# An encoder layer on one core: TensorE in source order through the projection, mixers in fewer visits, first gates fetched early

## The chip, the cores and the metric

The kernel runs on one core of one Trainium2 chip. The metric is device time in microseconds of one execution; lower is better. A core has five engines that each run their own list of instructions in order: TensorE (PE, matrix products and transposes, with PEld for the loads of the stationary operand), VectorE (DVE), ScalarE (ACT), GpSimd (POOL) and SyncE (SP, which here issues nearly all DMA transfers). They wait for each other by semaphores.

## The reference

One hybrid layer on T = 1024 tokens of width D = 1024, in float32. All weights are inputs.

```python
hn  = rms_norm(x, norm_mix_pre)
proj = hn @ w_in                       # a_qk a_v a_o a_gates | b_q b_k b_v b_r b_lr
# group A, 4 mLSTM heads: silu(dwconv3(a_qk)) gives q, k; gates i, f; one scan forward, one backward, summed
y_a = sigmoid(a_o) * head_rms_norm(h_fw + h_bw)
# group B, 4 GLA heads: decay per key dimension, log_sigmoid(b_lr @ gla_w2 + gla_b) / 16; forward and backward, summed
y_b = silu(b_r) * head_rms_norm(o_fw + o_bw)
x = x + rms_norm(concat(y_a, y_b) @ w_out, norm_mix_post)
hn = rms_norm(x, norm_ffn_pre)
g = dwconv3(hn @ w_gate, conv_w, conv_b)
x = x + rms_norm((gelu(g) * (hn @ w_up)) @ w_down, norm_ffn_post)
```

## The kernel before

**Stages.** Every float32 product is made of three float32r products of high and low halves (xh·wh, xl·wh, xh·wl). The program has four stages: the input is normalised and transposed, with a first small projection (`vacc`, L262); then the rest of the input projection with both mixers woven in; then the out-projection with the norms (`oacc`, L1002); then the gated MLP by Strassen-like products (`pr`, L1063 and L1221). The change is to the second stage alone, which begins at 47.4 us, after the eight transposes `sacc` (L283).

**The projection** is a generator, `proj`. Its unit is a block of 24 matmuls of 512 columns (`f_block`, tile `facc`, L171) or 48 matmuls of 256 columns (`t_block`, tile `tacc`, L182); a block yields after every 6 or 12 matmuls, and one such piece is called a step here. In order it makes the keys and queries of group B (`facc`), the second half of its values (`tacc`), queries and keys of group A with their convolution on ACT and DVE (`facc`), the values of group A (`tacc`), and then the two output gates, `in_gate` (`tacc`), which go to the DRAM arrays `dG` (tokens 0–511 and 512–1023). Weights come as `wraw` by SP and are split by ACT and DVE, one group of columns ahead (`ahead`). Flags in `done` ("bq", "bv", "aqk", "av", "gate") tell the mixers what is there.

**The mixers** are the other generator, `mix`. The sequence is cut into 8 chunks c of 128 tokens. `gla_decay` makes the decays of group B (8 matmuls `z`, L382, each from the split weights `w2r` and the rows `lrx`). `gate_rows` makes the gates of group A, and ends in transposes `ptc` (L373). `gla`: for each chunk `levels` forms the products of queries and keys inside it at eight distances L = 64, 32, 16, 8, 4, 2, 1, 0 (`sc`); for each level POOL makes exponents (`D`), ACT the exponential (`E`), DVE the weighted queries and keys (`Q`, `K`, `kz`), PE the small products, and DVE or ACT collects them (`acc`, `Pt`). `states` makes the running states (transpose `ptk`, product `U`, then DVE steps through `slots`, L537). `finish` makes the output of a chunk (`o`, L699 and L700), which ACT copies to `ob`, and SP stores to `dyb`. `mlstm` does the same for group A: `states` (load `kk`, transpose `ptm` L738, product `Um` L762, DVE steps `both_step`), `decays` (loads of `RB`, `RI`, then POOL and ACT), `front` (product `sr` L797, then DVE `RB` L798) and `back` (`nd`, L807 and L811; output stored to `dya`).

**The end of the stage.** After the last chunk `out_weights` loads the 8 row blocks of `w_out` (`oraw`, L862) through three buffers with the tags yv, yv, gv, and splits each on ACT and DVE (`woh`, `wol`). Then `prep(0)` loads the gated outputs of the first 128 tokens into buffers of the same tags (`yv` from `dya` and `dyb`, L875 and L876; `gv` from `dG`, L878), multiplies them on DVE (L882), and transposes them on PE (`pt`, L888), from which the out-projection starts.

**What sets the order.** Both generators only emit instructions; `_interleave` emits the next piece of the one that has run up less weight. The scheduler of the Tile framework then takes every engine's instructions, PE's too, by priority and by its own estimate of when their operands are ready, so that emitted order and final order differ. Pools of buffers (`ps` 3, `pe` 2 and `mm` 3 banks of PSUM, and pools in SBUF) add waits for a buffer's earlier readers.

Of the kernel before, what the change touches and what calls it, by code (L numbers as in the profile page):

```python
# [36 lines left out]
W_PROJ = 0.25  # L37
R_AUX, R_COLS, R_GLA, R_STATES, R_ML, R_OUT = 3.4, 0.6, 0.7, 0.7, 1.9, 2.0
# [4 lines left out]
def _interleave(*gens):  # L43
    live = [[g, w, 0.0] for g, w in gens]
    while live:
        e = min(live, key=lambda v: v[2])
        e[2] += e[1]
        try:
            w = next(e[0])
            if w is not None:  # L50
                e[1] = w
        except StopIteration:
            live.remove(e)
# [3 lines left out]
def tile_encoder_layer(  # L57
# [243 lines left out]

    def gate_rows():
# [26 lines left out]
        rm = rw.tile([R, NC, P], F32, name="rm")  # L329
        nc.gpsimd.memset(rb, 0.0)  # L330
# [38 lines left out]
        yield  # L369
        for c in range(NC):  # L370
# [4 lines left out]
            yield R_COLS * W_PROJ  # L375
        yield R_AUX * W_PROJ
# [93 lines left out]
    def in_gate(c0, off, silu):  # L470
        for g in range(2):
            wh, wl = ready.pop(0)
            yield
            for q in range(4):
# [10 lines left out]
                if q % 2:  # L485
                    nc.sync.dma_start(dG[q // 2].rearrange("(t p) n -> p t n", p=P)[:, :, off + 256 * g:off + 256 * g + 256], s)
                yield
# [11 lines left out]
    def mix():  # L499
        yield R_AUX * W_PROJ  # L500
        yield from gla_decay()
        yield from gate_rows()
        rctx.close()
        while "bq" not in done:
            yield
        gp = mctx.enter_context(tc.tile_pool(name="gp", bufs=2, reuse_waits="tile"))
        mslots = gp.tile([P, NC, H, P + 1], F32, name="mslots", bufs=1)
# [4 lines left out]

        nc.gpsimd.memset(mslots[:, 0], 0.0)
# [35 lines left out]
        def gla():  # L549
# [22 lines left out]

            def states():
                for c in range(NC):
                    S = lp.tile([P, H, P + 1], F32, name="S")
                    nc.sync.dma_start(S, dS[c // 4][c % 4])
                    kk = load(lp, "kk", dkk[c])
                    v = v_tile(lp, dvb, c)
                    nc.scalar.activation(gam[:, c, :], S[:, :, P], AF.Exp, scale=1.0 / TEMP)
                    E = edge_decay(S, hi, lo)  # L580
                    kd = w2k("Q", 3)
                    nc.vector.tensor_tensor(out=kd, in0=E, in1=kk, op=ALU.mult)
                    yield
                    pt = ps.tile([P, H, P], F32, name="ptk", tag="ps")
                    for h in range(H):
                        nc.tensor.transpose(pt[:, h, :], kd[:, h, :], ident)
# [268 lines left out]
    def out_weights():  # L855
# [11 lines left out]
        for _ in prep(0):  # L867
            pass
# [446 lines left out]
```

## Time and profile before

| | |
|---|---|
| median of 3 runs | 1193.14 us (1188.0 to 1194.34) |
| the profiled execution | 1189.67 us, span 1187.9 us |
| mean granted TensorE clock | 0.989 of full |
| PE busy | 1151.1 us, 97% of the span |
| DVE, ACT, POOL busy | 878.7, 591.4, 166.5 us |
| the stage that the change touches | 47.4 to 439.5 us |

The profile has one row for each group of instructions or, in its timeline, one for each instruction or run of like instructions: start in us, duration, engine, line, operation, `out<-in`, and in square brackets the idle time before it with what ended it. A matmul's row is longer than its pitch, since matmuls overlap: the distance of two starts is what one costs. "PEclk" is the clock that the throttle granted, where 1.00 is full.

### The profile page before, as it was taken

The page shows a single profiled execution, that of the slowest core. Times are in us where ns is not written, and L with a number is a line of the kernel's source. Part 1 is how long each engine was busy: PE and PEld are TensorE (multiplying, and loading weights), DVE is VectorE, ACT ScalarE, POOL GpSimd, SP SyncE. Part 2 cuts the span into 40 slices and gives each one's busy share as a digit, 9 for nine tenths or more (in the row PEclk, how much of TensorE's full clock was granted, in tenths as well). Part 3 has the DMA queues.
Part 4 walks back from the last instruction along what each step waited for, and adds up shares of the span by engine and source line. Part 5 has one row for each costly group of instructions (what it writes and reads, how often), then busy time and mean ns, then how long its engine had stood idle before and what let it go on. Part 6 is the DMA issues. An engine that isn't in the chain of part 4 may idle for free.

```text
span 1187.9 us, 21230 instructions
## 1 busy us (share of the span) xinstructions
PE 1151.1 (97%) x7896; PEld 979.7 (82%) x7896; DVE 878.7 (74%) x1604; ACT 591.4 (50%) x1271; POOL 166.5 (14%) x240
## 2 busy tenths in 40 slices
PE   8999999999999969999999999999999999999997
PEld 7989778888989968878788888888888878888885
DVE  5676669777433557667998888888888877987666
ACT  6572686878556534446543243433433245445451
POOL 1200425665054200101000000000000000000001
PEclk9999999999989989999999999999999999999999
DMA  7453675554777385542144342333224238754245
GB/s 201 149 134 102 169 223 155 152 171 127 189 197 209 117 278 186 178 141 80 36 142 142 109 132 64 113 123 108 89 81 133 98 123 299 252 178 133 81 137 190
DMA packets 134651, 175.77 MB, mean 148 GB/s; under 512 B 24964, under 2 KB 89860, under 8 KB 134548
## 3 DMA queue, kind: packets, MB, share of 16 engines
q1 hardware_dynamic: 134116, 172.58, 47.3%
q0 software_dynamic: 432, 1.84, 0.4%
q8 instruction: 62, 1.02, 0.3%
q14 instruction: 41, 0.34, 0.1%
HBM read 126.78 MB, written 47.53 MB: 147 GB/s over the span
## 4 chain that ended last, share of the span: by engine, by line
PE 73%; DVE 7%; ACT 6%; DMA 6%; issue 3%; POOL 3%; SPq 1%; DVEq 0%; POOLq 0%; ACTq 0%
PE pr L1063 35%; PE pr L1221 17%; PE facc L171 5%; PE oacc L1002 4%; PE tacc L182 4%; PE vacc L262 2%; DMA qq<-dmqq 1%; DMA yv<-dya 1%; DMA oraw<-in_w_out_dram 1%; DVE kz L637 1%; ACT sq L543 1%; DVE slots L537 1%; POOL RB L786 1%; POOL D L621 1%; POOL D L622 1%
## 5 line engine op out<-in xcount | busy, mean ns | idle before, releaser
L1063 PE MATMUL pr<-T,ah 128*128 128x512 f32 x704 | 217.2, 389 | 1.3 <-DVE G L1101 1.3
L1063 PE MATMUL pr<-B,ah 128*128 128x512 f32 x528 | 162.8, 390 | 0.0
L1063 PEld LDWEIGHTS pr<-T,ah 128*128 128x128 f32 x704 | 132.1, 188 | 29.4 <-DVE G L1101 1.8
L1063 PE MATMUL pr<-T,al 128*128 128x512 f32 x352 | 137.0, 389 | 0.0
L182 PE MATMUL tacc<-wh,xh 128*128 128x256 f32 x448 | 130.5, 291 | 0.0
L182 PE MATMUL tacc<-wl,xh 128*128 128x256 f32 x448 | 130.0, 290 | 0.0
L182 PE MATMUL tacc<-wh,xl 128*128 128x256 f32 x448 | 127.1, 284 | 0.0
L1221 PE MATMUL pr<-dwl,dah 128*128 128x512 f32 x308 | 120.0, 390 | 0.7 <-DVE dwl L113 0.7
L1221 PE MATMUL pr<-dwh,dal 128*128 128x512 f32 x308 | 120.1, 390 | 0.0
L1221 PE MATMUL pr<-dwh,dah 128*128 128x512 f32 x308 | 119.3, 390 | 0.0
L1063 PEld LDWEIGHTS pr<-B,ah 128*128 128x128 f32 x528 | 99.0, 188 | 20.4
L1063 PE MATMUL pr<-B,al 128*128 128x512 f32 x264 | 102.7, 389 | 0.0
L112 ACT CAST dah<-ar 128x512 fp32r<-128x512 f32 x77 | 47.6, 621 | 98.0 <-PE pr L1221 44.2
L182 PEld LDWEIGHTS tacc<-wh,xh 128*128 128x128 f32 x448 | 85.5, 191 | 2.7 <-issue 0.2
L182 PEld LDWEIGHTS tacc<-wl,xh 128*128 128x128 f32 x448 | 85.5, 191 | 1.4
L182 PEld LDWEIGHTS tacc<-wh,xl 128*128 128x128 f32 x448 | 85.7, 191 | 0.3
L112 ACT CAST ah<-fraw 128x512 fp32r<-128x512 f32 x64 | 39.6, 619 | 82.7 <-PE pr L1063 49.7
L113 DVE TENSOR_TENSOR dal<-ar,dah 128x512 fp32r<-128x512 f32 x77 | 53.0, 690 | 37.0 <-ACT dah L112 36.7
L1063 PEld LDWEIGHTS pr<-T,al 128*128 128x128 f32 x352 | 66.1, 188 | 13.6
L112 ACT CAST ah<-sa 128x512 fp32r<-128x512 f32 x44 | 27.4, 622 | 83.6 <-DVE sa L943 52.9
L1221 PEld LDWEIGHTS pr<-dwl,dah 128*128 128x128 f32 x308 | 57.8, 188 | 13.1 <-DVE dwl L113 1.1
L1221 PEld LDWEIGHTS pr<-dwh,dal 128*128 128x128 f32 x308 | 57.8, 188 | 12.9 <-DVE dal L113 0.9
(292 smaller groups left out, 2536.0 us busy)
## 6 DMA issues: line engine op xcount, KB each, us to landing
ar<-dA SPq DMA_DIRECT2D x77, 256.0 KB
wraw<-in_w_in_dram SPq DMA_DIRECT2D x48, 256.0 KB
fraw<-in_ffn_w_gate_dram SPq DMA_DIRECT2D x22, 512.0 KB
fraw<-in_ffn_w_up_dram SPq DMA_DIRECT2D x22, 512.0 KB
dA<-s SPq DMA_DIRECT2D x20, 512.0 KB
dA<-sx SPq DMA_DIRECT2D x10, 768.0 KB
Y<-in_ffn_w_down_dram SPq DMA_DIRECT2D x22, 256.0 KB
S<-dS SPq DMA_DIRECT2D x16, 258.0 KB
```

The lines of the kernel that those rows point to most:

```text
L112: nc.scalar.copy(out=hi, in_=src)
L113: nc.vector.tensor_tensor(out=lo, in0=src, in1=hi.bitcast(F32), op=ALU.subtract)
L171: nc.tensor.matmul(acc, w[:, k, cs], v[:, k, hs], start=(k == 0 and n == 0), stop=(k == NK - 1 and n == 2))
L182: nc.tensor.matmul(acc[:, i, :], v[:, k, ts], w[:, k, :], start=(k == 0 and n == 0), stop=(k == NK - 1 and n == 2))
L262: nc.tensor.matmul(acc, v[:, k, ts], w[:, k, :], start=(k == 0 and n == 0), stop=(k == NK - 1 and n == 2))
L537: nc.vector.scalar_tensor_tensor(out=sl[rs, o, h, :], in0=sl[rs, c, h, :], scalar=sc(c, h)[rs], in1=sl[rs, o, h, :], op0=ALU.mult, op1=ALU ...
L543: nc.scalar.activation(sq, o[:, h, :], AF.Square, accum_out=ss[:, h:h + 1])
L621: nc.gpsimd.tensor_tensor(out=dv[:, :, :, 0, :], in0=ref, in1=xv[:, :, :, 0, :], op=ALU.subtract)
L622: nc.gpsimd.tensor_tensor(out=dv[:, :, :, 1, :], in0=xv[:, :, :, 1, :], in1=ref, op=ALU.subtract)
L1002: nc.tensor.matmul(accs[hf], v[:, j, :], w[:, k, hf * 512:(hf + 1) * 512], start=(k == 0 and n == 0), stop=(k == NK - 1 and n == 2))
L1063: nc.tensor.matmul(acc, A[i][:, k, :], B[b][j][:, k, :], start=(k == 0 and n == 0), stop=(k == 3 and n == 2))
L1221: nc.tensor.matmul(accs[i], o[v][:, ts], o[w], start=(p == 0 and n == 0), stop=(p == NP - 1 and n == 2))
```

## The change

One: PE keeps source order through the projection. `_interleave` is called inside a block in which the scheduler leaves PE's instructions as they were emitted; the other engines are still scheduled. `_interleave` itself now takes the mixers as the main generator, and the projection as filler: each `yield n` of the mixers emits n steps of the projection, and what is left of the projection comes at the end. The constants F_* are these numbers.

Two: the mixers' products come in fewer, fuller visits. In `gla` the levels go in pairs (64, 32), (16, 8), (4, 2), (1, 0), each pair prepared one visit ahead, and the output of a chunk (`finish`) is made one visit after its last pair, in the visit of the next chunk's second pair; `states` makes U of one chunk and the transpose of the next in one visit. In `mlstm` `back(c)` and `front(c+1)` share a visit, the first two `decays` are called among the states, and the values are loaded in `front`. The steps of `gate_rows` are woven between those of `gla_decay`, and its transposes are in `gate_cols`. The buffers `Q` go from 3 to 6, `KT` from 1 to 2, and `mslots` moves to the pool of `mlstm`.

Three: a new flag, "half", is set once the gates of the first 512 tokens are stored, and `out_weights` starts the loads and products of `prep(0)` then, instead of after all gates.

```diff
-def _interleave(*gens):
...
+def _interleave(main, filler):
+    due = 0.0
+    for n in main:
+        due += n
+        while due >= 1.0:
+            next(filler, None)
+            due -= 1.0
+    for _ in filler:
+        pass
...
+F_DECAY, F_GATES, F_COLS, F_AUX = 2.6, 10.0, 1.0, 3.0
+F_STATES, F_GLA, F_MSTATES, F_ML, F_OUT = 2.0, 1.6, 1.4, 4.4, 2.0
...
     def mix():
-        yield R_AUX * W_PROJ
-        yield from gla_decay()
-        yield from gate_rows()
+        gates_ = gate_rows()
+        for n, _ in enumerate(gla_decay()):
+            if n % 2 == 0:
+                next(gates_, None)
+            yield F_DECAY
+        for _ in gates_:
+            pass
+        yield F_GATES
+        yield from gate_cols()
         rctx.close()
+        yield F_AUX
...
+            def stream(cs, last, fill=F_GLA):
+                emit = None
+                prepare = chunk(cs[0])
+                for c in cs:
+                    for n in range(4):
+                        if n == 1 and c > 0:
+                            finish(c - 1)
+                        if emit:
+                            emit()
+                        emit = prepare(n)
+                        if n == 2 and c < cs[-1]:
+                            prepare_next = chunk(c + 1)
+                        yield fill
+                    if c < cs[-1]:
+                        prepare = prepare_next
+                emit()
+                yield fill
+                if last:
+                    finish(cs[-1])
+                    yield F_GLA
...
-            yield from levels(0)
+            yield from stream([0], False, 2.6)
             while "bv" not in done:
-                yield
+                yield 1
             yield from states()
-            for c in range(NC):
-                if c + 1 < NC:
-                    yield from levels(c + 1)
-                yield from finish(c)
+            yield from stream(list(range(1, NC)), True)
             lctx.close()
...
                     if n % 2 and n > 1:
                         both_step(n // 2)
-                    yield
+                    if n in (3, 5):
+                        decays(n // 4)
+                    yield F_MSTATES
                 for j in range(NC // 2, NC - 1):
                     both_step(j)
-                    yield
...
             yield from states()
-            decays(0)
-            decays(1)
-            yield R_ML * W_PROJ
             front(0)
+            yield F_ML / 2
             for c in range(NC):
                 if c + 2 < NC:
                     decays(c + 2)
+                back(c)
                 if c + 1 < NC:
                     front(c + 1)
-                yield
-                back(c)
-                yield
+                yield F_ML
...
-            yield
+            yield F_OUT
+        nc.sync.dma_start(gpost, rows_of(a["norm_mix_post"][0]))
+        while "half" not in done:
+            yield 1
+        first = prep(0)
+        next(first)
         while "gate" not in done:
-            yield
-        for _ in prep(0):
+            yield 1
+        for _ in first:
             pass
-        nc.sync.dma_start(gpost, rows_of(a["norm_mix_post"][0]))
...
-    _interleave((proj(), W_PROJ), (mix(), 1.0))
+    with tc.manual_schedule(engines={mybir.EngineType.PE}):
+        _interleave(mix(), proj())
```

**PE, where the stage begins**, behind the transposes `sacc`. `z` is the first decay product, which reads the split weights `w2r`; `facc` belongs to the projection. Before:

```order
L283 MATMUL sacc<-ident,sml 112x128 x8
L171 MATMUL facc<-xh,wh 128x512
L171 MATMUL facc<-xl,wh 128x512
L171 MATMUL facc<-xh,wl 128x512
...
L171 MATMUL facc<-xh,wl 128x512
L382 MATMUL z<-lrx,w2r 128x512 x2
```

Now:

```order
L281 MATMUL sacc<-ident,sml 112x128 x8
L385 MATMUL z<-lrx,w2r 128x512
L169 MATMUL facc<-xh,wh 128x512
L169 MATMUL facc<-xl,wh 128x512
L169 MATMUL facc<-xh,wl 128x512
...
L385 MATMUL z<-lrx,w2r 128x512
```

Before, 48 `facc` matmuls stand between `sacc` and the first `z`; now the first `z` comes directly behind `sacc`, and the 6 `facc` of the first step stand between it and the second.

**PE, between the two mixers**: `o` is the output of the last GLA chunk, `ptm` the first transpose of the mLSTM keys, `tacc` the projection. Before:

```order
L699 MATMUL o<-v,Pt 128x128
L700 MATMUL o<-slots,qd 128x128
L182 MATMUL tacc<-wl,xh 128x256
L182 MATMUL tacc<-wh,xl 128x256
L182 MATMUL tacc<-wh,xh 128x256
...
L182 MATMUL tacc<-wh,xh 128x256
L738 MATMUL ptm<-ident,kk 128x64 x4
```

Now:

```order
L180 MATMUL tacc<-wh,xl 128x256
L721 MATMUL o<-v,Pt 128x128
L722 MATMUL o<-slots,qd 128x128
...
L722 MATMUL o<-slots,qd 128x128
L779 MATMUL ptm<-ident,kk 128x64 x4
L180 MATMUL tacc<-wh,xh 128x256
```

Before, 57 `tacc` matmuls (not all shown) stand between the last `o` and `ptm`; now none does. On SP the load `kk` that `ptm` reads stands behind the store `dyb` of that last `o`, before and now; now two loads `wraw` stand between them as well.

**SP, at the end of the stage**: loads of `w_out` (`oraw`), stores of the gates (`dG`), then the first loads of `prep(0)` (`gv`, `yv`). Before:

```order
L862 DMA oraw<-in_w_out_dram 128x1024 x2
L486 DMA dG_67<-stg 128x4x256
L862 DMA oraw<-in_w_out_dram 128x1024 x3
L921 DMA fcw<-in_ffn_conv_wt_dram 128x66
L878 DMA gv<-dG_67 128x1024
L875 DMA yv<-dya_77 128x512
L486 DMA dG_68<-stg 128x4x256
L876 DMA yv<-dyb_69 128x512
```

Now:

```order
L898 DMA oraw<-in_w_out_dram 128x1024 x3
L489 DMA dG_67<-stg 128x4x256
L898 DMA oraw<-in_w_out_dram 128x1024
L918 DMA gv<-dG_67 128x1024
L915 DMA yv<-dya_77 128x512
L916 DMA yv<-dyb_69 128x512
L915 DMA yv<-dya_78 128x512
```

The loads of the first tokens stand behind the last `oraw` in both; the last store of gates, `dG_68`, which stood between them, now comes later. Over the stage PE's list has as many matmuls of every kind as before; the alternations between the projection and other work fall from 219 to 141, and 228 instead of 180 `tacc` matmuls stand behind the last mixer product.

More of the change, by code (lines that the diff above doesn't have):

```diff
@@ L571, in gla @@
             lo, hi = slice(0, 64), slice(64, 128)
-            def states():
-                for c in range(NC):
[L575 to L582, printed above, removed]
-                    yield
-                    pt = ps.tile([P, H, P], F32, name="ptk", tag="ps")
-                    for h in range(H):
-                        nc.tensor.transpose(pt[:, h, :], kd[:, h, :], ident)
-                    KT = w2k("KT", 1)
-                    nc.scalar.copy(out=KT, in_=pt)
-                    yield
-                    U = ps.tile([P, H, P], F32, name="U", tag="ps")
-                    for h in range(H):
-                        nc.tensor.matmul(U[:, h, :], KT[:, h, :], v[:, h, 0:P], start=True, stop=True)
-                    state_out(slots, c, [(0, H, U)])
-                    if 1 <= c < NC - 1:
-                        state_step(slots, lambda c, h: gam[:, c, h:h + 1], c, 0)
-                    yield
@@ new lines, in states @@
+            def states():
+                nxt = keys(0)
+                yield F_STATES
+                prev = None
+                for c in range(NC + 1):
+                    if prev is not None:
+                        b, KT, v = prev
+                        U = ps.tile([P, H, P], F32, name="U", tag="ps")
+                        for h in range(H):
+                            nc.tensor.matmul(U[:, h, :], KT[:, h, :], v[:, h, 0:P], start=True, stop=True)
+                        state_out(slots, b, [(0, H, U)])
+                        if 1 <= b < NC - 1:
+                            state_step(slots, lambda c, h: gam[:, c, h:h + 1], b, 0)
+                        prev = None
+                    if c < NC:
+                        kd, v = nxt
+                        pt = ps.tile([P, H, P], F32, name="ptk", tag="ps")
+                        for h in range(H):
+                            nc.tensor.transpose(pt[:, h, :], kd[:, h, :], ident)
+                        KT = w2k("KT")
+                        nc.scalar.copy(out=KT, in_=pt)
+                        prev = (c, KT, v)
+                        if c + 1 < NC:
+                            nxt = keys(c + 1)
+                    yield F_STATES
@@ L848, in mix @@
         mid_ctx.close()
-        yield R_OUT * W_PROJ
+        yield F_OUT
         yield from out_weights()
```

99 lines of the change are left out of this document (47 added, 52 removed).

## The prediction

> **What bounds the kernel now.** First the page: the busy shares, and the chain of work that ended last.
>
> ```profile
> PE 1151.1 (97%) x7896; PEld 979.7 (82%) x7896; DVE 878.7 (74%) x1604; ACT 591.4 (50%) x1271; POOL 166.5 (14%) x240
> ...
> PE 73%; DVE 7%; ACT 6%; DMA 6%; issue 3%; POOL 3%; SPq 1%; DVEq 0%; POOLq 0%; ACTq 0%
> ```
>
> PE is busy 97% of the span and carries 73% of the chain, so an idle gap of PE that is closed, or opened, counts in full. What other engines do counts only where PE waits for it. Next the busy time by stretch, for the woven stage up to its last mixer product, and for the GLA loop in it (columns: length, then PE, PEld, DVE, ACT, POOL busy, granted clock, DMA share).
>
> ```profile
> 47.38:408.96 361.58, 348.70 (x4151) 309.69 (x4148) 233.16 (x539) 231.49 (x594) 142.15 (x198) 0.99 0.57 161
> ```
>
> ```profile
> 180.00:300.00 120.00, 114.14 (x2357) 104.43 (x2358) 95.93 (x222) 89.39 (x241) 71.10 (x109) 1.00 0.51 150
> ```
>
> In the woven stage PE is idle 361.58 − 348.70 = 12.9 us; nothing else there can be won except by cheaper PE work. In the GLA loop DVE is busy 80%, PE 95%. The waits of PE (total, times, longest) name the gaps:
>
> ```profile
> PE pt L888 <- DVE yv L882: 8.9, 2, 8.7
> PE sc L656 <- DVE kz L637: 3.8, 5, 1.2
> PE nd L807 <- DVE RB L798: 3.1, 2, 2.9
> PE sc L652 <- DVE K L632: 1.7, 1, 1.7
> ```
>
> The largest, 8.7 us, lies at the stage's end and waits for the first gated tokens. A gap can also cost more than its length:
>
> ```profile
> 320.00:340.00 20.00, 17.06 (x120) 15.93 (x121) 7.65 (x21) 9.87 (x27) 10.31 (x5) 0.87 1.00 228
> 340.00:360.00 20.00, 20.00 (x171) 19.02 (x170) 7.90 (x33) 12.79 (x45) 7.71 (x6) 0.96 0.58 162
> ...
> 440.00:460.00 20.00, 19.33 (x79) 15.44 (x79) 10.05 (x28) 5.88 (x12) 0.45 (x1) 0.81 0.78 243
> ```
>
> ```profile
> 334.13 1.53 PE L807 MATMUL nd<-v,RB 128*128 128x129 f32 x8 [2.94 <-DVE RB L798]
> 335.58 2.08 PE L797 MATMUL sr<-qq,kko 64*128 64x128 f32 x8
> 337.59 2.09 PE L807 MATMUL nd<-v,RB 128*128 128x129 f32 x8
> ```
>
> ```profile
> 344.70 1.16 PE L797 MATMUL sr<-qq,kko 64*128 64x128 f32 x8
> 345.78 0.39 PE L182 MATMUL tacc<-wh,xh 128*128 128x256 f32 x1
> 346.00 0.28 PE L182 MATMUL tacc<-wl,xh 128*128 128x256 f32 x1
> 346.12 0.28 PE L182 MATMUL tacc<-wh,xl 128*128 128x256 f32 x1
> ```
>
> After the gap of 2.94 us the same eight `sr` take 2.01 us (335.58 to 337.59) instead of 1.08 (344.70 to 345.78), and the granted clock of two stretches is 0.87 and 0.96: 0.13 × 20 + 0.04 × 20 = 3.4 us of PE's time lost. After the 8.7 us gap it is 0.81 over 20 us, 3.8 us. I take 3.5 us for each such gap. The gap of 1.7 us (`K`) lies in the stretch 180 to 300, where the clock is 1.00: so short a gap doesn't do it.
>
> **What the change removes.** (1) The idle of 12.9 us and the lost clock of 3.5 us in the stage: PE's list is new throughout, so I count both as gone and price the new gaps below. (2) Alternations on PE between projection and mixers, 219 before, 141 now. Coming back costs 0.22 us for the first `tacc` (345.78 to 346.00) where the next costs 0.12, so 0.10 more; with the facc rows below it is 0.34 (48.22 to 48.56) against 0.22, 0.12 more. Going out should cost about the same. 78 × 0.105 = 8.2 us; the lower bound counts only the returns, 4.1. (3) 228 instead of 180 `tacc` stand behind the last mixer product: 48 × 0.12 = 5.8 us that no longer precede it. Since the end hangs on that product (below), this counts. Together 12.9 + 3.5 + 8.2 + 5.8 = 30.4 us (26 to 31).
>
> **What it adds.** *A, the start.* PE keeps `z` directly behind `sacc`, and `z` needs the split weights `w2r`.
>
> ```profile
> 48.22 0.49 PE L171 MATMUL facc<-xh,wh 128*128 128x512 f32 x1
> 48.56 0.39 PE L171 MATMUL facc<-xl,wh 128*128 128x512 f32 x1
> 48.78 0.40 PE L171 MATMUL facc<-xh,wl 128*128 128x512 f32 x1
> ```
>
> ```profile
> 53.19 0.44 SPq L291 DMA_DIRECT2D w2b<-in_gla_b_dram  x1
> ```
>
> ```profile
> 55.53 0.69 DVE L293 TENSOR_TENSOR w2r<-w2b,w2r 33x512 fp32r<-33x512 f32 x1 [2.20 <-ACT w2r L292]
> ```
>
> The last load of `w2b` is issued at 53.19, `w2r` is whole at 56.22, and PE is free at 48.22. Before, 48 `facc` (11 us) covered this. Now nothing does: 8.0 us idle, plus 3.5 of clock, 11.5 us. Nothing ahead of these loads changes, so this is the surest term (8.0 if the clock holds, 12 at most).
>
> *B, the first GLA products.* They need `K` of chunk 0, which follows the last `ptc`:
>
> ```profile
> 119.58 0.50 PE L171 MATMUL facc<-xh,wh 128*128 128x512 f32 x1
> ```
>
> ```profile
> 129.94 0.68 DVE L632 TENSOR_TENSOR K<-E,kk 128x512 f32<-128x512 f32 x1
> ```
>
> From 119.58 to 130.6 it is 11.0 us; the new order puts 6 `facc` and 60 `tacc` there, 6 × 0.23 + 60 × 0.12 = 8.6 us: 2.4 us (0 to 5).
>
> *C, the first `o`* needs all 24 backward steps of the states on DVE.
>
> ```profile
> 188.61 1.50 DVE L537 SCALAR_TENSOR_TENSOR slots<-slots,gam 64x128 f32<-64x128 f32 x5
> ```
>
> At 0.30 us a step they take 7.2 us, with weights of the next chunk and convolution work on the same engine some 9; cover is 24 `facc`, 5.5 us: 3.5 us (1 to 9).
>
> *D, the GLA loop.* PE now waits at each pair, in order, for what DVE made one visit earlier, and `o` stands one visit behind the last pair.
>
> ```profile
> L637 DVE TENSOR_TENSOR kz<-E,kk 64x256 f32<-64x256 f32 x70 | 29.2, 416 | 0.5
> L629 DVE TENSOR_TENSOR Q<-E,qq 128x512 f32<-128x512 f32 x42 | 28.9, 688 | 5.5 <-ACT E L624 5.0
> L671 DVE COPY_PREDICATED acc<-bmask,sc 128x128 f32<-128x128 uint32 x35 | 10.4, 298 | 0.5
> ```
>
> ```profile
> L688 ACT COPY Pt<-acc 32x128 f32<-32x128 f32 x28 | 8.2, 293 | 2.8 <-DVE acc L671 2.6
> ```
>
> These three DVE groups are 68.5 us over 7 chunks, 9.8 a chunk; the whole stretch is 95.9 / 7 = 13.7 with the projection's share, against a pace of PE of some 14. On average it fits; in the chunks that hold convolutions or splits it doesn't, by 1 to 3 us. In four chunks only 12 `tacc` (1.4 us) cover the way from the last `sc` to `o`, which takes two `acc` (0.6) and four `Pt` copies (1.2) with their handovers: about 1 us each. I take 7 us, near the 5.5 that the waits for `kz` and `K` cost now; 4 if all else hides, 17 if DVE or its feeders set the pace of each chunk (2.4 us × 7).
>
> *E, between the mixers.* `ptm` stands directly behind the last `o`; its operand `kk` is loaded behind the store `dyb`, which waits for ACT's copy of that `o`.
>
> ```profile
> 297.42 0.59 ACT L702 COPY ob<-o 128x512 f32<-128x512 f32 x1 [0.40 <-DMA dyb<-ob]
> ```
>
> ```profile
> 295.31 3.06 SPq L547 DMA_DIRECT2D dyb<-ob  x2
> 298.46 0.45 SPq L734 DMA_DIRECT2D kk<-dmk  x1
> ```
>
> The copy takes 0.6 us; the issues on SP (`dyb` 0.4, two `wraw`, `kk`) some 1.6; from the last issue of a load to its reader it is 2.4 us at the stage's end (`yv`, issued until 436.63, read at 439.03, rows below). With 0.2 for the handovers 4.8 us, which 57 `tacc` (6.9 us) covered before. With the clock 8.3 us (3 to 10). [...]
>
> *G, the first `nd`* waits for `RB` behind 16 state steps; 36 `tacc` and `sr` cover some 5.8 us: 1.5 us (0 to 3), where it is 2.9 now. The states of both mixers and the seams between the blocks: 2 us (0 to 5).
>
> Sum of what is added: 11.5 + 2.4 + 3.5 + 7 + 8.3 + 1.5 + 2 = 36.2 us.
>
> **The end, and the early fetch.**
>
> ```profile
> 408.96 0.39 PE L182 MATMUL tacc<-wh,xh 128*128 128x256 f32 x1
> ...
> 430.53 0.28 PE L182 MATMUL tacc<-wh,xl 128*128 128x256 f32 x1
> 439.49 1.22 PE L888 MATMUL pt<-ident,yv 128*128 128x128 f32 x4 [8.68 <-DVE yv L882]
> ```
>
> ```profile
> 433.88 0.33 SPq L878 DMA_DIRECT2D gv<-dG  x1
> 435.12 0.33 SPq L875 DMA_DIRECT2D yv<-dya  x1
> ...
> 436.13 0.50 SPq L876 DMA_DIRECT2D yv<-dyb  x1
> ```
>
> ```profile
> 439.03 1.14 DVE L882 SCALAR_TENSOR_TENSOR yv<-gv,hr,yv 128x128 f32<-128x128 f32 x4 [1.76 <-DMA yv<-dya]
> ```
>
> The last mixer product ends at 408.96, the first transpose `pt` starts 30.5 us later. The fetch is the tail of a chain: 8 loads `oraw` through three buffers that `yv` and `gv` share, so `yv` can be loaded only when the seventh is split. The change moves the call of `prep(0)`, not these buffers; on SP its loads stand behind the last `oraw` as before, and only one store of gates (0.4 us) no longer stands between. So `pt` comes about 30.1 us after the last mixer product, a gain of 0.4. PE's remaining 228 `tacc` (27.4 us) now end 2.8 us ahead of it instead of 8.7; whether the clock drops after 2.8 us is open (3.5 us), and I count half, 1.7. [...]
>
> **Sum:** −30.4 + 36.2 − 0.4 − 1.7 = +3.7 us on the profiled 1189.67, so 1193.4. The median of the runs is 3.5 above the profiled one: 1197 us.
>
> **The rivals.** *Slower: DVE sets the pace of the GLA loop.* With PE in order, a late `kz` holds up the projection behind it too, where the scheduler's order went around it. The point from which it decides is a DVE load, including convolutions, above PE's 14 us a chunk; for it speaks 13.7 us on average, against it that ACT and POOL are far from full and that each pair has a visit of lead. Price: D becomes 17 and C 6, +12.5: 1209 us. *Faster: the new gaps are short.* If the lead of a visit covers B, C, D and G to 3 us together (for it: six buffers `Q` instead of three), and A and E stay, the sum is 11.4 lower: 1186 us; if E's load also comes early, 1180. *The early fetch does what it says*, and `pt` follows the `tacc` without a gap: 2.8 + 1.8 less than forecast, 1192, still no change that can be told; against it stands the chain of buffers. *The order isn't kept*, and it stays at 1193: PE's list as shown speaks against it.
>
> **How the numbers follow.** The forecast and its near cases hold 0.4, DVE at the bound or longer gaps than priced 0.3, short gaps 0.25, the rest 0.05. A measurement of this kernel tells about 0.5%, 6 us, from no change: below 1187 counts as faster (0.27), above 1199 as slower (0.34), between as the same (0.39). The range, 1178 to 1211, goes from short gaps with an early load to DVE at the bound; the forecast's own is 1189 to 1204.
>
> **What would show it.** A: the first `z` with 8 us of idle before it and a clock of 0.5 behind. E: `ptm` waiting about 5 us for `kk`. D: `sc` waiting for `kz`, `K` or `Q` in most chunks, together 5 to 9 us, and `o` for `Pt`. The end: `pt` about 30 us after the last `nd`, waiting for `yv`. The forecast is wrong if `z` starts without that gap, if the load of `kk` is issued before the last `dyb`, or if the GLA loop's waits are far from 7 us.

## The result, and the profile after

The changed kernel takes 1224.62 us (median of 4 runs, 1222.11 to 1226.27) against 1190.91 us before (median of 4): a ratio of 1.028, 95% interval 1.0241 to 1.0319. It is 33.7 us slower, where 1197 us and no change that can be told were forecast: +3.7 us on the change, and +33.7 measured. The profiled execution took 1222.11 us, its span is 1220.3 us.

The page of the changed kernel, busy shares and chain, against 97% and 73% for PE before:

```profile
PE 1150.7 (94%) x7896; PEld 986.0 (81%) x7896; DVE 885.5 (73%) x1604; ACT 593.7 (49%) x1271; POOL 165.7 (14%) x240
...
PE 71%; DVE 10%; DMA 7%; ACT 6%; issue 3%; POOL 2%; SPq 1%; DVEq 0%; POOLq 0%; ACTq 0%
```

The woven stage up to its last mixer product, by the same view as before (length, PE, PEld, DVE, ACT, POOL busy, granted clock, DMA share):

```profile
47.24:442.81 395.57, 345.02 (x4103) 311.58 (x4100) 239.58 (x538) 233.54 (x593) 140.88 (x198) 0.95 0.53 146
```

The stage is 395.6 us long instead of 361.6. PE is idle in it for 395.57 − 345.02 = 50.6 us, where it was 12.9, and its clock is 0.95 instead of 0.99. The waits of PE over 2.5 us:

```profile
PE ptm L779 <- DMA kk<-dmk: 8.2, 1, 8.2
PE z L385 <- DMA gf<-gst: 8.2, 1, 8.2
PE o L721 <- ACT Pt L712: 7.9, 5, 2.5
PE sc L675 <- DVE kz L656: 7.0, 5, 3.1
PE nd L848 <- ACT sq L551: 3.8, 2, 2.0
PE z L385 <- DVE dA L394: 3.7, 1, 3.7
PE nd L848 <- DVE RB L839: 3.5, 1, 3.5
PE o L722 <- DVE slots L545: 3.3, 1, 3.3
PE pt L928 <- DVE yv L922: 2.9, 1, 2.9
PE sc L663 <- DVE Q L646: 2.7, 1, 2.7
```

Before, one line of this view was over 4 us (`pt`), and it lay at the stage's end. Now ten are over 2.6 us, and nine of them lie in the stage's middle. (Two names in this view mislead. For the first `z` it gives a load that `z` doesn't read; its operand `w2r` is whole at 55.61 + 0.69 = 56.30, and `z` starts at 56.51. In e4_finish and e11_seamfill, where the start is the same, the view names `w2r`, 8.0 us. For `nd` behind `sq` see below, under the mLSTM visits.)

```profile
55.61 0.69 DVE L291 TENSOR_TENSOR w2r<-w2b,w2r 33x512 fp32r<-33x512 f32 x1 [2.42 <-ACT w2r L290]
```

```profile
56.51 0.77 PE L385 MATMUL z<-lrx,w2r 98*128 98x512 f32 x1 [8.23 <-DMA gf<-gst]
82.86 0.47 PE L385 MATMUL z<-lrx,w2r 98*128 98x512 f32 x1 [3.70 <-DVE dA L394]
```

The stage's end stands as it did: from the first `tacc` behind the last mixer product (442.81) to the first `pt` (473.29) it is 30.5 us, as before. So all of the loss lies ahead of that product.

```profile
442.81 0.39 PE L180 MATMUL tacc<-wh,xh 128*128 128x256 f32 x1
```

```profile
473.29 1.49 PE L928 MATMUL pt<-ident,yv 128*128 128x128 f32 x5 [2.87 <-DVE yv L922]
```

**A ledger.** The rest of this text uses three sums over a trace, taken from the first `sacc` to 20 us behind the first `oacc`: the idle time of PE; the lost clock, that is half of PE's busy time in the stretches for which the trace records the clock at half; and the number of alternations on PE (unbroken runs of matmuls under one output tile's name). What is left of the span from the first `sacc` (at some 47 us) on, without the idle time and the lost clock, is the work.

| kernel | span | idle | lost clock | alternations | work |
|---|---|---|---|---|---|
| before | 1187.9 | 22.2 | 7.0 | 256 | 1111 |
| changed | 1220.3 | 53.8 | 18.0 | 188 | 1101 |

The difference of 32.4 us is +31.6 of idle, +11.0 of lost clock and −10 of work. The holes and their clock cost four times what the work falls by. That the fewer alternations save these 10 us fits the 8.2 us forecast, but isn't shown: the ledger over all kernels, at the end of the experiments, has 1099 to 1106 us of work at 185 to 197 alternations. And most of the fall in alternations is the order's, not the fuller visits': the kernel before has 197 under source order.

### The profile page after: what moved, and what is told of

Read it like the earlier page. It is cut to its first block, busy times and chain, and to the rows that moved or that the text cites. A ratio compares the mean times of both kernels' runs of the same rounds, so it can differ in the third digit from the quotient of the medians.

```text
span 1220.3 us, 21210 instructions
## 1 busy us (share of the span) xinstructions
PE 1150.7 (94%) x7896; PEld 986.0 (81%) x7896; DVE 885.5 (73%) x1604; ACT 593.7 (49%) x1271; POOL 165.7 (14%) x240
## 4 chain that ended last, share of the span: by engine, by line
PE 71%; DVE 10%; DMA 7%; ACT 6%; issue 3%; POOL 2%; SPq 1%; DVEq 0%; POOLq 0%; ACTq 0%
PE pr L1104 32%; PE pr L1262 16%; PE tacc L180 7%; PE oacc L1043 4%; PE facc L169 4%; DMA yv<-dya 1%; DMA wraw<-in_w_in_dram 1%; DMA oraw<-in_w_out_dram 1%; PE nd L848 1%; DMA RB<-drr 1%; ACT sq L551 1%; DVE T L111 1%; DVE slots L545 1%; PE o L721 1%; DVE kz L656 1%
## 5 line engine op out<-in xcount | busy, mean ns | idle before, releaser
L1104 PEld LDWEIGHTS pr<-T,ah 128*128 128x128 f32 x704 | 132.1, 188 | 29.4 <-DVE G L1142 1.7
L180 PE MATMUL tacc<-wh,xh 128*128 128x256 f32 x448 | 133.3, 297 | 0.0
L111 DVE TENSOR_TENSOR dal<-ar,dah 128x512 fp32r<-128x512 f32 x77 | 52.8, 688 | 37.1 <-ACT dah L110 35.8
L1262 PEld LDWEIGHTS pr<-dwh,dah 128*128 128x128 f32 x308 | 57.8, 188 | 13.0 <-ACT dah L110 1.1
```

The source lines that it names most:

```text
L111: nc.vector.tensor_tensor(out=lo, in0=src, in1=hi.bitcast(F32), op=ALU.subtract)
L180: nc.tensor.matmul(acc[:, i, :], v[:, k, ts], w[:, k, :], start=(k == 0 and n == 0), stop=(k == NK - 1 and n == 2))
L1104: nc.tensor.matmul(acc, A[i][:, k, :], B[b][j][:, k, :], start=(k == 0 and n == 0), stop=(k == 3 and n == 2))
L1262: nc.tensor.matmul(accs[i], o[v][:, ts], o[w], start=(p == 0 and n == 0), stop=(p == NP - 1 and n == 2))
```

## The experiments

Two theories were set against each other from the start. *Holes*: PE in source order stands still wherever its next operand isn't there, and a hole costs clock besides. *Bursts* or *pace*: the new visits load the other engines so that the time is lost under any order, or a closed hole opens again elsewhere. Where no interval is given there is one time for each kernel; kernels that ran together had one time of the kernel before beside them (1190.1, 1193.0 and 1189.9 us in the first three groups). In a later group the kernel before, run 18 times, took 1187.1 to 1200.6 us. So a difference of a few us between two single times says little by itself; there the reading rests on the waits and the sums of the trace, which are of one execution each.

### PE's order given back to the scheduler

```diff
-    with tc.manual_schedule(engines={mybir.EngineType.PE}):
-        _interleave(mix(), proj())
+    _interleave(mix(), proj())
```

> The changed kernel with PE's order left to the scheduler again; the fuller visits and the early fetch stay. Theory 'holes' (PE in source order stands still where its next operand isn't there, and a hole of over some 2.5 us costs about 3.4 us of clock besides): the scheduler moves projection work into the holes, PE's idle before the last mixer product falls from 50.6 us to 10 to 20, and the time is 1180 to 1197 us. Rival 'bursts' (the fuller visits load DVE, ACT and POOL in bursts, and the time is lost under any order of PE): idle stays above 35 us and the time above 1208 us.

Measured: 1197.3 us, idle 29.5 us in the ledger (25.9 of it ahead of the last mixer product), lost clock 9.6. So source order costs some 27 us of the 34, and the new visits with the early fetch lose 6 to 7 us on top even when the scheduler places them (idle 29.5 against 22.2, lost clock 9.6 against 7.0). The time is at the edge of what 'holes' gave, the idle 6 us above it: both theories have a share, the first the larger one. The waits that are left:

```profile
PE z L385 <- DVE dA L394: 5.0, 2, 4.7
PE nd L848 <- ACT sq L551: 4.6, 2, 3.7
PE pt L928 <- DVE yv L922: 3.1, 1, 3.1
...
PE o L721 <- ACT Pt L712: 2.5, 5, 1.2
```

The first `z`, `ptm`, `kz` and `Q` are gone from the top of the list; `z` on `dA` and the `nd` are not.

### Source order alone, on the kernel before

```diff
-    _interleave((proj(), W_PROJ), (mix(), 1.0))
+    with tc.manual_schedule(engines={mybir.EngineType.PE}):
+        _interleave((proj(), W_PROJ), (mix(), 1.0))
```

> The kernel before with only PE's instructions left in the order in which they are emitted; old weights, old visits, old fetch. Theory 'order' (keeping source order is what costs, because each short hole that the scheduler filled stays open): PE's idle before the last mixer product rises from 12.9 us to over 35, and the time is over 1212 us. Rival 'new visits' (the holes come from how the new visits are cut, and source order alone does little): idle under 25 us, 1186 to 1202 us.

Measured: 1211.3 us, idle ahead of the last mixer product 37.1 us, the whole ledger 44.8 and 12.5. Source order by itself costs 18 to 20 us on the old visits, in the order in which they happen to be emitted, which settles the first question for 'order' (the time is 1 us under its bound, the idle 2 us over its own). With the run above this gives a square: old visits 1191 (scheduler) and 1211 (source order), new visits 1197 and 1224.6. The cost of the order is 20 and 27, that of the new visits 6 and 13.

### Cover for the first decay product

```diff
+        yield 8
         gates_ = gate_rows()
-F_DECAY, F_GATES, F_COLS, F_AUX = 2.6, 10.0, 1.0, 3.0
+F_DECAY, F_GATES, F_COLS, F_AUX = 2.6, 2.0, 1.0, 3.0
```

> The changed kernel with 8 steps of the projection (48 facc) ahead of the first z, and 8 steps fewer behind the gate rows (F_GATES 2 instead of 10), so that as much projection as before is left at the end. Theory 'holes': the first z no longer waits (8.2 us) and the half clock behind it goes (3.4 us); 1222 becomes 1209 to 1213 us. Rival 'pace' (a hole that is closed opens again at the next place, since the gates' scans on DVE set the time up to the transposes ptc): ptc or the next z wait 6 us or more, and the time is 1217 to 1223 us.

Measured: 1218.0 us. The first `z` no longer waits; but the next hole widens (`z` on `dA` 4.8 instead of 3.7), `ptc` waits 1.0, and the first `sc` on `Q` and `K` 4.6 and 2.0 instead of 2.7 and 0.5. Idle ahead of the last mixer product falls by 2.5 us only (50.6 to 48.1). 'Pace' was nearer here (its one wait of 6 us or more didn't come, the loss is spread over four places): the projection that covers the first hole was taken from behind the gate rows, and was cover there too.

### The first mLSTM keys loaded early

```diff
+    kk0 = mid.tile([DK, H, P], F32, name="kk0")
...
+                        if n == 0 and c == NC - 1:
+                            nc.sync.dma_start(kk0, dmk[0])
...
-                kk = lp.tile([DK, H, P], F32, name="kk")
-                nc.sync.dma_start(kk, dmk[c])
+                kk = kk0
+                if c != 0:
+                    kk = lp.tile([DK, H, P], F32, name="kk")
+                    nc.sync.dma_start(kk, dmk[c])
```

> The changed kernel with the keys kk of the first mLSTM chunk loaded while the last GLA chunk is at work, into a buffer of their own; PE's order is the same. Theory 'holes': ptm no longer waits (8.2 us) and the half clock behind it goes (3.4 us): 1209 to 1213 us. Rival 'pace': the first Um waits for its values v, which are still loaded behind the last dyb, 4 us or more, and the time is 1214 to 1220 us.

Measured: 1226.1 us, no gain, and 50.5 us of idle as in the changed kernel. The first `ptm` follows `o` without a wait, but the hole moves to the next two loads of the same queue:

```profile
PE ptm L784 <- DMA kk<-dmk: 5.8, 1, 5.8
PE Um L805 <- DMA v<-dva: 3.7, 1, 3.7
```

That the time is above the rival's is the lost clock, 24.3 us in the ledger against 18.0. In the changed kernel the rows of ACT and SP show where the 8.2 us go, instead of 4.8. The copy `ob` ends at 316.19, `dyb`, two `wraw` and `kk` are issued by 318.32, and then the DMA engines are full (share 1.01) until `ptm` can start at 323.43:

```profile
315.61 0.58 ACT L724 COPY ob<-o 128x512 f32<-128x512 f32 x1
```

```profile
316.21 0.33 SPq L555 DMA_DIRECT2D dyb<-ob  x1
316.63 1.17 SPq L148 DMA_DIRECT2D wraw<-in_w_in_dram  x2
317.85 0.47 SPq L775 DMA_DIRECT2D kk<-dmk  x1
```

```profile
318.40:323.40 5.00, 0.00 (x0) 0.00 (x0) 0.69 (x1) 0.62 (x1) 1.45 (x5) 0.64 1.01 225
```

From the end of the issue to the reader it is 5.1 us here, where 2.4 was taken. That the full DMA engines make the difference is the likely reason, and isn't shown: no run issues this load with the engines idle.

### Cover between the mixers instead

```diff
             while "aqk" not in done or "av" not in done:
                 yield 1
+            yield 5
-F_STATES, F_GLA, F_MSTATES, F_ML, F_OUT = 2.0, 1.6, 1.4, 4.4, 2.0
+F_STATES, F_GLA, F_MSTATES, F_ML, F_OUT = 2.0, 1.6, 1.4, 3.8, 2.0
```

> Of the former, only the 60 tacc between the last o and ptm and the smaller F_ML. Theory 'holes': ptm's wait of 8.2 us falls to under 2, the half clock there goes, and the time is 1210 to 1215 us. Rival 'pace': the loads behind it (v, RB) are still late, Um, ptm or nd wait as long as ptm did, and the time is 1218 to 1226 us.

Measured: 1221.8 us. `ptm` waits 0.4 us instead of 8.2, and idle ahead of the last mixer product falls to 44.8; but 12 `tacc` more stand ahead of that product, `pt` waits 4.7 us instead of 2.9, and no lost clock is saved (18.3 against 18.0 in the ledger). The hole was closed as 'holes' has it; the time was the rival's (1218 to 1226).

### The output of a GLA chunk one visit later

```diff
-                        if n == 1 and c > 0:
+                        if n == 2 and c > 0:
```

> The changed kernel with the output o of a GLA chunk made one visit later (in the visit of the next chunk's third pair instead of its second). Theory 'holes': o no longer waits for Pt (7.9 us in five waits) and E no longer stands behind ob on ACT, so the waits for kz and Q fall too; PE's idle in the GLA loop falls from 16 us to under 7, and with two or three half clocks fewer the time is 1204 to 1214 us. Rival 'pace' (DVE's and ACT's work per chunk sets the pace of the loop): the same idle turns up under the names kz, K and Q, and the time is 1218 to 1224 us.

Measured: 1218.1 us. No `o` waits for `Pt` any more (7.9 us before), the stretch from the last `U` to the last chunk's `o` takes 127 us instead of 133, and idle ahead of the last mixer product falls by 6.3 us, from 50.6 to 44.3. But one wait on `Q` grows to 5.4, and the lost clock takes 4.8 us back (22.8 in the ledger); the time is at the rival's edge (1218 to 1224). The way from the last `sc` over `acc` and `Pt` to `o` was a cause of its own; the waits for DVE remained:

```profile
PE sc L663 <- DVE Q L646: 8.6, 3, 5.4
...
PE sc L675 <- ACT sq L551: 3.0, 1, 3.0
```

### Three covers together, under source order

The first `z`, the later `o` and the cover between the mixers in one kernel (the three edits above).

> The changed kernel, PE in source order, with the cover dealt out anew and the same work: 48 facc ahead of the first z, 8 steps fewer behind the gate rows, o one visit later, 60 tacc between the last o and ptm, taken from the mLSTM visits (F_ML 3.8 instead of 4.4). Theory 'holes': the first z, o and ptm no longer wait, idle before the last mixer product falls from 50.6 to about 33 us and the clock loss from 14.7 to about 9, and the time is 1198 to 1206 us. Rival 'pace': what is closed opens elsewhere (z on dA, sc on Q, nd on RB), idle stays above 42 us and the time is 1212 to 1222 us.

Measured: 1208.8 us, idle ahead of the last mixer product 39.2 us, lost clock 15.5 in the ledger. It is 13 to 16 us better than the changed kernel, nearly half of the 34, and lies between the two theories' numbers: about half of the idle that the three places had stays closed, the rest opens as `Q` (10.6 us), `dA` (4.8) and `nd`.

```profile
PE sc L664 <- DVE Q L647: 10.6, 3, 5.4
PE z L385 <- DVE dA L394: 4.8, 1, 4.8
```

### The buffers at the stage's end, and the early fetch

The tags of the eight `oraw` become ya, yb, gv, ya, yb, gv, yb, yb, those of `yv` and `om` ya and yb in turn, and the first tokens are fetched after the sixth block:

```diff
-            raw = op.tile([P, D], F32, name="oraw", tag=("yv", "yv", "gv")[k % 3], bufs=(2, 2, 1)[k % 3])
+            raw = op.tile([P, D], F32, name="oraw", tag=("ya", "yb", "gv", "ya", "yb", "gv", "yb", "yb")[k], bufs=1)
...
+            if k == 5:
+                while "half" not in done:
+                    yield 1
+                first = prep(0)
+                next(first)
```

> The changed kernel with the buffers at the stage's end dealt out anew, of the same total size: the last two blocks of w_out go through one buffer, so that those for the first gated tokens are free earlier, and their loads are asked for after the sixth block. Theory 'buffers' (the early fetch does nothing because its buffers come free last): the first pt comes 27.3 to 28.5 us after the last mixer product instead of 30.5, where the tacc end, and the time falls from 1222 to 1218 to 1220 us. Rival (the transfers themselves are late, whatever the buffers): 30 us or more, 1221 to 1225 us.

> The kernel before with the same two edits: buffers dealt out anew, and the first tokens fetched once the first 512 gates are stored, after the sixth block of w_out. Here only 21.9 us of tacc stand behind the last mixer product. Theory 'buffers': the first pt comes 24 to 27 us after it instead of 30.5, the hole of 8.7 us shrinks by 4 to 6, and the time falls from 1190 to 1181 to 1187 us. Rival (transfers at their pace): 29.5 us or more, 1188 to 1192 us.

Measured: 1226.2 us on the changed kernel, and 1191.0 us on the kernel before; the first `pt` comes 29.6 and 29.4 us behind the last mixer product, instead of 30.5 each. So about 1 us, and 'buffers' falls as the whole cause. On the changed kernel the idle time falls by 3.6 us, and the lost clock takes 3.0 of it back. In the second run the loads of `yv` are issued at 433.05, but `gv` stands on SP behind the seventh block, which now waits for the one buffer it has:

```profile
433.05 0.33 SPq L883 DMA_DIRECT2D yv<-dya  x1
433.42 0.43 SPq L884 DMA_DIRECT2D yv<-dyb  x1
436.51 0.33 SPq L864 DMA_DIRECT2D oraw<-in_w_out_dram  x1
...
439.10 0.33 SPq L886 DMA_DIRECT2D gv<-dG  x1
```

The early fetch stays limited by the queue of eight loads and the buffers together; whether room for all of them would help wasn't tried.

### The gate rows behind the decays again, under the scheduler

```diff
-        gates_ = gate_rows()
-        for n, _ in enumerate(gla_decay()):
-            if n % 2 == 0:
-                next(gates_, None)
+        for _ in gla_decay():
             yield F_DECAY
-        for _ in gates_:
+        for _ in gate_rows():
             pass
```

> The changed kernel with PE's order left to the scheduler, and the gate rows emitted after the decay products, as before, instead of between them. Theory (the four scans of the gate rows on DVE, 9 us, hold up the decays that z's buffers wait for): the wait of z for dA, 5.0 us, goes, with the half clock behind it, and 1197 becomes 1189 to 1193 us. Rival 'pace': the gates come later by as much, ptc or the first sc wait instead, and the time is 1196 to 1199 us.

Measured: 1201.4 us, against 1197.3 with the woven gates, and above both ranges; idle is 32.7 instead of 29.5 in the ledger, lost clock 11.5 instead of 9.6. `z` no longer waits for `dA`, and `ptc` waits 7.2 us for the gates instead. Why `dA` was late is seen in the changed kernel's DVE, where four scans of the gate rows, 9 us, stand ahead of it:

```profile
72.40 2.25 DVE L336 TENSOR_TENSOR_SCAN rb<-rmask,gf 4x1024 f32<-4x1024 f32 x1
...
79.05 2.25 DVE L337 TENSOR_TENSOR_SCAN rm<-gf,gi 4x1024 f32<-4x1024 f32 x1
81.32 0.68 DVE L393 SCALAR_TENSOR_TENSOR dA<-z,dD 64x512 f32<-64x512 f32 x1
```

The scans have to be done before `ptc`; woven in they delay `z`, behind they delay `ptc`. The weaving is not what the new visits lose by.

### The mLSTM visits cut as before, under the scheduler and under source order

`states`, the loop over the chunks and `decays` are those of the kernel before, with rates of 0.74 and 2.2 steps a visit:

```diff
-                back(c)
                 if c + 1 < NC:
                     front(c + 1)
-                yield F_ML
+                yield 2.2
+                back(c)
+                yield 2.2
```

> The changed kernel with PE's order left to the scheduler and with the mLSTM visits cut as before (front of the next chunk and back of this one apart, decays of the first chunks after the states, values loaded with the decays). Theory 'mLSTM visits' (of the 7 us that the new visits lose under a free order, most comes from the merged mLSTM visits, where nd waits 9 us for RB and for hs): these waits fall to 4 us or less and 1197 becomes 1189 to 1193 us. Rival 'GLA visits and gates': the waits of nd stay or other waits of that size appear, 1195 to 1200 us.

> The changed kernel, PE in source order, with only the mLSTM visits cut as before. If the merged mLSTM visits cost the same under source order as under the scheduler (8 us between two runs there), 1222 becomes 1212 to 1217 us. If under source order other holes hide that (the old cut has more visits for PE to stand still at), it stays at 1219 to 1228 us.

Measured: 1189.2 us under the scheduler, beside 1189.9 of the kernel before, and 1223.5 us under source order. Under the scheduler no `nd` waits over 0.3 us, and 8 us come back: so the new visits' loss there is the merged mLSTM visits (the edit also moves the loads of `v` and the first `decays`; which of these it is wasn't taken apart), and the GLA visits, the gates and the early fetch together neither cost nor gain. How a merged visit waits is seen in e1_free, from POOL to ACT to DVE to PE:

```profile
392.52 2.40 POOL L826 TENSOR_TENSOR RB<-RB,cin 128x1024 f32<-128x1024 f32 x1 [9.86 <-DMA RB<-drr]
```

```profile
394.95 2.16 ACT L830 ACTIVATE RB<-RB,cols 128x128 f32<-128x128 f32 x7 [5.33 <-POOL RB L826]
```

```profile
397.62 0.69 DVE L487 SCALAR_TENSOR_TENSOR stg<-stg,tacc 128x512 f32<-128x512 f32 x1 [7.81 <-ACT stg L483]
```

```profile
400.93 1.22 DVE L839 SCALAR_TENSOR_TENSOR RB<-sr,RB 128x1024 f32<-128x1024 f32 x1
```

```profile
402.25 3.78 PE L848 MATMUL nd<-v,RB 128*128 128x129 f32 x16 [3.72 <-ACT sq L551]
```

The load of `RB` comes late; ACT stands at its exponentials, a gate (`stg`) stands behind them, DVE stands at that gate for 7.8 us, and behind it on DVE stand the work on the last `nd`, which was done by 392, and the product `RB` (L839) that the next `nd` reads. That product ends at 402.15, and `nd` starts 0.1 us later; the `sq` that the view names had ended at 401.56. In the changed kernel it is the same: the two `nd` put down to `sq` (3.8 us) start 0.1 us behind this product, which stands behind the `hs` of the chunk before.

Under source order the same edit also takes the waits of `nd` away, idle ahead of the last mixer product falls from 50.6 to 44.0, and yet nothing is gained: 192 instead of 228 `tacc` are left behind the last mixer product, and `pt` waits 7.6 us instead of 2.9. The 36 `tacc` that moved ahead of that product are 4.3 us (0.12 each), most of the 6.6 that the holes gave back; what covered there lacked at the end.

### Versions meant to beat both

Gate rows behind the decays with 15 steps behind them, mLSTM visits as before at 1.9 steps, order by the scheduler:

> PE's order left to the scheduler, the new GLA visits and the early fetch kept, the mLSTM visits cut as before, the gate rows behind the decays as before but with 15 instead of 10 steps of projection behind them (and 1.9 instead of 2.2 a visit in mLSTM). A version meant to beat both. Theory 'holes': the wait of z for dA (4.9 us and a half clock) goes and ptc finds its rows ready behind the longer cover, so 1189 becomes 1180 to 1185 us. Rival 'pace': the wait turns up at ptc or in the mLSTM loop, 1187 to 1193 us.

Measured: 1196.8 us, ratio to before 1.0037 (1.0023 to 1.0052). `ptc` still waits 4.2 us, and the clock is at half over 17 us behind it (101.1 to 118.2): slower, as the rival had it and more.

e9_free_oldml with 1.75 instead of 2.2 steps a visit, so that 288 `tacc` are left for the end; and the kernel before with R_ML 1.45 instead of 1.9:

> e9_free_oldml with less projection between the mLSTM visits (1.75 steps a visit instead of 2.2), so that 288 instead of 192 tacc stand behind the last mixer product. There the first pt waits 7.1 us for the gated tokens, and in the mLSTM loop no wait is over 0.3 us. Theory 'ledger' (the time is the work plus all idle of PE plus the lost clock; projection taken from a place with no wait and put where PE waits is a gain): the last mixer product comes 11 us earlier, pt waits for nothing, the time falls from 1189 to 1178 to 1183 us. Rival 'pace' (the mLSTM chunks can't go faster, nd or sr wait for RB, qq or hs instead): 1186 to 1191 us.

> The kernel before with the same done by its own number (R_ML 1.45 instead of 1.9): 252 instead of 180 tacc behind the last mixer product, where pt waits 8.7 us. Theory 'ledger': 1191 becomes 1180 to 1185 us. Rival 'pace': nd waits more for RB and hs than it does now (3.8 us), 1188 to 1193 us.

Measured: the first takes 1186.1 us, ratio 0.9953 (0.9929 to 0.9977), and beats both kernels, by 0.5% and 3%; the second 1192.8 us, ratio 1.0006 (0.9983 to 1.003). In the first the last mixer product comes at 404.13 instead of 412.26, and PE waits 1.95 us ahead of `pt` instead of 7.1:

```profile
404.13:441.00 36.87, 34.92 (x291) 34.74 (x289) 16.20 (x29) 15.21 (x26) 1.01 (x1) 1.00 0.65 218
```

Against e9_free_oldml, from which it differs in this alone, idle and lost clock fall from 30.1 to 25.3 us and the span by 3.3, about a third of the gain that the ledger allowed (7 us of idle and 3 of clock): `sr` and `nd` wait 3.5 us that they did not there. Where the gain over the kernel before comes from isn't shown: from the first `sacc` to the first `oacc` it is 394.5 us here and 394.0 before, and what the profiled execution gains, 3.7 us of span, lies behind that, where the code is the same; over the 17 traces that part alone takes from 741 to 748 us. In the second the loop couldn't be shortened at all (its trace is of one of its slower executions, 1196.3 us): `nd` waits 4.2 for `RB` and `sr` up to 2.1 for its loads, and the last mixer product is 8 us later than in the kernel before.

The ledger over the kernels (us; one profiled execution each):

| kernel | order | span | idle | lost clock | alternations | work |
|---|---|---|---|---|---|---|
| before | scheduler | 1187.9 | 22.2 | 7.0 | 256 | 1111 |
| e7_before_slots | scheduler | 1189.2 | 19.9 | 10.7 | 256 | 1111 |
| e15_before_ml15 | scheduler | 1194.5 | 23.1 | 11.9 | 254 | 1112 |
| e5_old_order | source | 1209.5 | 44.8 | 12.5 | 197 | 1105 |
| changed | source | 1220.3 | 53.8 | 18.0 | 188 | 1101 |
| e2_start | source | 1216.2 | 50.8 | 15.0 | 191 | 1103 |
| e3_seam | source | 1224.4 | 54.0 | 24.3 | 189 | 1100 |
| e4_finish | source | 1216.3 | 47.0 | 22.8 | 189 | 1099 |
| e6_slots | source | 1224.4 | 50.2 | 21.0 | 188 | 1106 |
| e10_covered | source | 1207.1 | 43.7 | 15.5 | 186 | 1101 |
| e11_seamfill | source | 1220.0 | 49.5 | 18.3 | 185 | 1104 |
| e13_order_oldml | source | 1221.7 | 51.7 | 17.0 | 191 | 1106 |
| e1_free | scheduler | 1195.5 | 29.5 | 9.6 | 221 | 1109 |
| e8_free_gates | scheduler | 1199.6 | 32.7 | 11.5 | 221 | 1108 |
| e9_free_oldml | scheduler | 1187.5 | 23.0 | 7.1 | 225 | 1110 |
| e12_mixed | scheduler | 1196.7 | 27.7 | 11.3 | 219 | 1110 |
| e14_free_ml18 | scheduler | 1184.2 | 21.2 | 4.1 | 225 | 1111 |

The work differs by 13 us over all rows, while idle and lost clock together go from 25 to 78 us: they decide the time. The work is 1108 to 1112 us under the scheduler and 1099 to 1106 in source order; within either group it doesn't follow the alternations.

## Why the prediction was wrong

**What held.** The work is 10 us lower in the ledger, where 8.2 us were forecast for the alternations; that they are the reason isn't shown (above). The 48 `tacc` moved behind the last mixer product: the 228 stand there, and hang on the same chain. A: 8.0 us of idle forecast, 8.2 measured, with a half clock behind. B: 2.4 against 2.7 + 0.5. C: 3.5 against 3.3. The end: `pt` 30.1 us behind the last mixer product forecast, 30.5 measured, the hole ahead of it 2.8 against 2.9, and the early fetch gave nothing. That 2.9 us did cost clock (half from 473.42 to 480.25), of which half was counted.

**The step that failed** is the sum of what the change adds, 36.2 us, with its terms D, E, G and "2 us for the rest", and the clock that was counted behind A and E alone. Idle was 29.2 of that sum, and is 50.6; clock was 7, and is 14.7 ahead of the last mixer product. The two differences are 29 us; the miss is 30.0 us on the change (33.7 against 3.7) and 27.6 on the time (1224.6 against 1197).

- D, the GLA loop: 7 us forecast, with bounds of 4 and 17; 16.0 measured (all idle between the first `o` and the last, without C). The estimate took the four short covers at 1 us each and stayed "near the 5.5 that the waits for `kz` and `K` cost now". But those 5.5 us were what the scheduler left over after placing projection into each gap; they were no measure of the gaps. That the order was the cause is shown by e1_free: by the scheduler, with the same visits, the waits for `Pt`, `kz`, `K` and `Q` fall from 18 us to 6.
- E: 4.8 us of idle forecast, 8.2 measured. The chain was right, the price of its last link was taken from another place: the load needs 5.1 us here, not 2.4, and the issues ahead of it 2.1 instead of 1.6.
- G: 1.5 forecast, 3.5 measured.
- Not priced, beyond the 2 us for the rest: `z` waiting for `dA` behind the scans (3.7), and `nd` waiting in the mLSTM loop for the product behind `hs` (3.8), both from edits that were read as regroupings without cost. For the second, e1_free and e9_free_oldml show that the edit to the mLSTM visits takes it away; the first only moves to `ptc` when undone.
- The clock: the forecast let only A and E cost it. In the trace eight places ahead of the last mixer product are followed by a half clock: A, `dA`, B, C, two in the GLA loop, E and G. Each costs 1.6 to 2.8 us, less than the 3.5 taken, since a part of the half clock falls into the hole (at E 3.6 of its 6.8 us, 319.82 to 323.43) or it lasts 3.4 us only (behind `dA`, 84.30 to 87.72); A and E together cost 3.6 instead of 7. So the price was too high and the count far too low.

The range was too narrow by its own terms. Their upper bounds (12, 5, 9, 17, 10, 3 and 5) add up to 61 us, which gives 1222; but the range stopped at one mechanism, 1211, as if the terms were independent. They weren't: with the order given back (e1_free) the idle time falls from 50.6 to 25.9 us, at D, E, A and B together.

**The rivals.** The slower one, DVE at its bound in the GLA loop, gave 1209 us and named the wrong cause. From the last `U` to the last chunk's `o` the loop takes 133 us now, and DVE is busy for 103 of them, 78% where it was 80%; the waits are on `Pt` (7.9 us) as much as on `kz` (7.0). In e1_free, the second row, the scheduler gets the same 103 us of DVE work done in 120.5 us, so DVE wasn't at its bound.

```profile
180.12:313.24 133.12, 113.77 (x2269) 101.39 (x2268) 103.31 (x231) 87.38 (x231) 71.33 (x108) 0.96 0.42 119
168.63:289.13 120.50, 112.86 (x2270) 98.30 (x2268) 103.21 (x231) 86.99 (x233) 73.45 (x108) 1.00 0.49 142
```

The case that was missing is the plain one: source order by itself, with no single mechanism, costs 18 to 20 us (e5_old_order), since short gaps that the scheduler filled stay open. The prediction gave "longer gaps than priced" a share of its 0.3, and no time.

## What to carry to other kernels

When a scheduler's order is replaced by a written one, the idle time that its trace shows is what is left after filling; price each wait anew, from the producer's end to the place where the consumer now stands, and not by the old waits. Work that fills holes is finite: cover that is added in one place lacks in another, and the gain comes where it is taken from a place without a wait (e14_free_ml18 gained a little on e9_free_oldml; e2_start and e11_seamfill lost most of theirs at the next places). An idle sum and a lost-clock sum over the trace tell such versions apart better than any single wait.

## What the runs showed of the hardware

A hole need not be long to cost clock, and its length alone doesn't decide. In the changed kernel one of 2.01 us is followed by a half clock, and one of 2.46 us is not:

```profile
227.52 0.69 PE L721 MATMUL o<-v,Pt 128*128 128x128 f32 x2 [2.01 <-ACT Pt L712]
```

```profile
297.44 0.49 PE L721 MATMUL o<-v,Pt 128*128 128x128 f32 x2 [2.46 <-ACT Pt L712]
```

The granted clock behind the two (length and PE busy are the first two numbers, the granted clock is the third from the end):

```profile
227.66:231.07 3.41, 3.41 (x16) 3.24 (x16) 2.45 (x5) 1.04 (x2) 0.00 (x0) 0.50 0.53 148
```

```profile
297.40:302.00 4.60, 4.55 (x77) 4.33 (x78) 2.76 (x6) 3.56 (x11) 0.04 (x1) 1.00 0.19 67
```

Between 47 and 500 us the changed kernel's trace has eleven holes of 1.9 us or more. Nine of them, 2.01 to 8.25 us long, have a clock of 0.50 behind them, over stretches of 3.4 or 6.8 us; that of 2.46 and one of 1.96 us (405.07 to 407.03) have 1.00. So the 2.5 us that the expectation of e1_free took as the least length of a costly hole, an estimate of the author's, doesn't hold: what a hole cost is read from the granted clock of the stretch behind it.
